# A mixture-of-experts kernel: TensorE in two short loops over fixed buffers, and results behind the weights

## The chip, the cores and the metric

The kernel runs on one core of one Trainium2 chip. The metric is the device time of one execution in microseconds (us); a profile adds the span of one execution, from its first to its last instruction, and shows what each engine did in it. In the profile PE is the matrix engine (TensorE), PEld its weight loads, DVE the vector engine, ACT the scalar engine, POOL the GpSimd engine and SP the sync engine. DMA transfers are issued by SP or by POOL and carried out by 16 DMA engines that the core has. Transfers that change the number type (float32 in memory, bfloat16 on the core) are issued by POOL here; they stand one behind another in POOL's ring. SP's transfers have a queue of their own.

## The reference

There are 8 experts. Each has 256 rows of x with 512 elements, a first weight of 512 x 2048 and a second of 2048 x 512, all float32:

```python
h = np.matmul(x, w1)      # (8, 256, 512) x (8, 512, 2048)
h = np.maximum(h, 0)
return np.matmul(h, w2)   # (8, 256, 2048) x (8, 2048, 512)
```

Each weight of an expert has 4.19 MB in memory. The 16 weights and x are 71.30 MB to read, the results 4.19 MB to write.

## The kernel before, in words

All matmuls are in bfloat16 and sum in float32. The weights are converted by the DMA that loads them. x must stand with its 512 elements on the partitions, so TensorE transposes it (line 88), and DVE and ACT copy the transposed blocks out of PSUM (lines 99 and 101).

*x.* `GROUPS` (line 35) divides the experts into four groups of 1, 1, 2 and 4. Experts 0 and 1 are loaded as float32 on SP (line 146, tile `x_f`) and cast by ACT (lines 156 and 157); groups 2 and 3 are loaded with a cast on the POOL ring (line 66, tile `x_b`). The transposes of a group stand shortly ahead of its first use; those of the last group stand between the quarters of expert 2's first layer (line 172).

*An expert.* `first_layer` (lines 103 to 123) makes the hidden layer in four quarters of 16 matmuls (line 111). Each quarter fills a PSUM tile `pt_h`, and ACT or DVE, in turn, evicts it with the relu into `ht_sb` (lines 121 and 119). `second_layer` (lines 125 to 139) has 32 matmuls of 512 columns (line 131) into two PSUM tiles `pt_o`; DVE evicts one and ACT the other into `out_sb` (lines 138 and 139), which holds the results of all experts.

*Weights.* `load_w1` (line 70) and `load_w2` (line 76) put one transfer of 4.19 MB each on the POOL ring, into pools of three buffers for w1 and three for w2 (`WB`, line 31). The second weights of experts 6 and 7 are loaded in two pieces each, so that the second layer can begin on the first piece.

*The order.* `manual_schedule` (line 49) keeps the written order on each engine; the framework sets the waits. Lines 145 to 194 are that order. Up to expert 4 the layers alternate; then the first layers of experts 5, 6 and 7 come together (lines 186 and 187), and their second layers after them (lines 192 and 193). On the ring the weights follow the same order: the last ones are w1 of experts 5, 6 and 7, then w2 of 5, 6 and 7 (lines 173 to 183).

*Results.* Result 0 is written in pieces: SP writes partitions 100 to 127 in five small transfers in mid-run (lines 169 and 170), POOL writes partitions 0 to 99 (line 191). Results 1 to 4 are one transfer on the ring (line 142, issued at line 190), so it stands behind the last weights. Results 5 to 7 are one transfer on SP at the very end (line 194), after the evictions of expert 7.

Of the kernel before, what the change touches and what calls it, by code (L numbers as in the profile page):

```python
# [7 lines left out]


@with_exitstack  # L10
def kernel(
    ctx: ExitStack,
    tc: tile.TileContext,
    x: bass.AP,
    w1: bass.AP,
    w2: bass.AP,
    out: bass.AP,
):
    nc = tc.nc
    P = 128  # L20
    bf = mybir.dt.bfloat16
    f32 = mybir.dt.float32
    relu = mybir.ActivationFunctionType.Relu

    E, C, H = x.shape
    F = w1.shape[2]
    MT = C // P
    KT1 = H // P
    KT2 = F // P
    FB = 4  # L30
    WB = 3
    CUTS = (100, 112, 116, 120, 124, 128)


    GROUPS = ((0, 1), (1, 1), (2, 2), (4, 4))


    w1_r = w1.rearrange("e (p kt) n -> e p kt n", p=P)
    w2_r = w2.rearrange("e (p kt) n -> e p kt n", p=P)
    out_r = out.rearrange("e (p mt) n -> p e mt n", p=P)  # L40

    const = ctx.enter_context(tc.tile_pool(name="const", bufs=1))
    wpool = ctx.enter_context(tc.tile_pool(name="weights", bufs=WB))
    hpool = ctx.enter_context(tc.tile_pool(name="hidden", bufs=3))
    ps_h = ctx.enter_context(tc.tile_pool(name="ps_h", bufs=2, space=bass.MemoryType.PSUM))
    ps_o = ctx.enter_context(tc.tile_pool(name="ps_o", bufs=4, space=bass.MemoryType.PSUM))


    ctx.enter_context(tc.manual_schedule())

    w1_sb, w2_sb, ht = {}, {}, {}
    group_of = {e: g for g, (e0, n) in enumerate(GROUPS) for e in range(e0, e0 + n)}
    x_f = const.tile([P, 2, MT, H], f32, name="x_f")
    x_b = [const.tile([P, n * MT, H], bf, name=f"x_b{g}") for g, (_, n) in enumerate(GROUPS)]
    xt = [const.tile([P, KT1, MT, n * P], bf, name=f"xt{g}") for g, (_, n) in enumerate(GROUPS)]
    o_sb = const.tile([P, E, MT, H], f32, name="out_sb")
    identity = const.tile([P, P], bf, name="identity")

    def x_rows(g):
        e0, n = GROUPS[g]  # L60
        return x[e0:e0 + n].rearrange("e c k -> (e c) k").rearrange(
            "(p j) k -> p j k", p=P
        )

    def load_x(g):
        nc.gpsimd.dma_start(x_b[g][:], x_rows(g))  # L66

    def load_w1(e):
        w1_sb[e] = wpool.tile([P, KT1, F], bf, tag="w1", name="w1_sb")
        nc.gpsimd.dma_start(w1_sb[e][:], w1_r[e])  # L70

    def load_w2(e):
        w2_sb[e] = wpool.tile([P, KT2, H], bf, tag="w2", name="w2_sb")
        cuts = {E - 2: (0, 8, 16), E - 1: (0, 9, 16)}.get(e, (0, KT2))
        for lo, hi in zip(cuts, cuts[1:]):
            nc.gpsimd.dma_start(w2_sb[e][:, lo:hi, :], w2_r[e, :, lo:hi, :])  # L76

    def transpose_x(g, blocks=None):


        n = GROUPS[g][1]
        J = n * MT
        KB = 8 // J
        for b in blocks if blocks is not None else range(KT1 // KB):
            pt = ps_o.tile([P, KB, J, P], bf, tag="ps_o", name="pt_tr")
            for i in range(KB):
                for j in range(J):
                    nc.tensor.transpose(  # L88
                        pt[:, i, j, :], x_b[g][:, j, b * KB + i::KT1], identity[:]
                    )  # L90
            for i in range(KB) if n > 1 else (slice(0, KB),):
                if n > 1:
                    src = pt[:, i].rearrange("p (l m) q -> p l m q", m=MT)
                    dst = xt[g][:, b * KB + i].rearrange("p m (q l) -> p l m q", l=n)
                    flip = b * KB + i
                else:
                    src, dst, flip = pt[:, i], xt[g][:], g
                if flip % 2:
                    nc.scalar.copy(dst, src)  # L99
                else:  # L100
                    nc.vector.tensor_copy(dst, src)  # L101

    def first_layer(e, between=()):
        g = group_of[e]
        i0 = (e - GROUPS[g][0]) * P
        ht[e] = hpool.tile([P, KT2, C], bf, tag="ht", name="ht_sb")
        for q in range(KT2 // FB):
            ph = ps_h.tile([P, FB, C], f32, tag="ps_h", name="pt_h")
            for i in range(FB):
                for kt in range(KT1):  # L110
                    nc.tensor.matmul(  # L111
                        ph[:, i, :],
                        w1_sb[e][:, kt, FB * q + i::KT2],
                        xt[g][:, kt, :, i0:i0 + P],
                        start=(kt == 0),
                        stop=(kt == KT1 - 1),
                    )
            if q % 2:
                nc.vector.tensor_relu(ht[e][:, FB * q:FB * (q + 1), :], ph[:])  # L119
            else:  # L120
                nc.scalar.activation(ht[e][:, FB * q:FB * (q + 1), :], ph[:], relu)  # L121
            if between:
                between.pop(0)()

    def second_layer(e):
        po = [
            ps_o.tile([P, H], f32, tag="ps_o", name=f"pt_o{mt}") for mt in range(MT)
        ]
        for kt in range(KT2):
            for mt in range(MT):  # L130
                nc.tensor.matmul(  # L131
                    po[mt][:],
                    ht[e][:, kt, mt * P:(mt + 1) * P],
                    w2_sb[e][:, kt, :],
                    start=(kt == 0),
                    stop=(kt == KT2 - 1),
                )
        nc.vector.tensor_copy(o_sb[:, e, 0, :], po[0][:])  # L138
        nc.scalar.copy(o_sb[:, e, 1, :], po[1][:])  # L139

    def store(e0, e1):
        nc.gpsimd.dma_start(out_r[:, e0:e1], o_sb[:, e0:e1])  # L142


    for e in (0, 1):
        nc.sync.dma_start(x_f[:, e], x_rows(e))
    load_w1(0)
    make_identity(nc, identity)
    load_w2(0)
    load_x(2)  # L150
    load_w1(1)
    load_w2(1)
    load_x(3)
    load_w1(2)
    load_w2(2)
    nc.scalar.copy(x_b[0][:], x_f[:, 0])  # L156
    nc.scalar.copy(x_b[1][:], x_f[:, 1])  # L157
    transpose_x(0)

    first_layer(0)  # L160
    load_w1(3)
    transpose_x(1)
    second_layer(0)
    load_w2(3)
    first_layer(1)
    load_w1(4)
    transpose_x(2)
    second_layer(1)
    for p, q in zip(CUTS, CUTS[1:]):
        nc.sync.dma_start(out_r[p:q, 0], o_sb[p:q, 0])  # L170
    load_w2(4)
    first_layer(2, [lambda kt=kt: transpose_x(3, [kt]) for kt in range(KT1)])
    load_w1(5)
    second_layer(2)
    first_layer(3)
    load_w1(6)
    second_layer(3)
    first_layer(4)
    load_w1(7)
    load_w2(5)  # L180
    load_w2(6)
    second_layer(4)
    load_w2(7)


    for e in (5, 6, 7):
        first_layer(e)


    store(1, 5)  # L190
    nc.gpsimd.dma_start(out_r[:CUTS[0], 0], o_sb[:CUTS[0], 0])  # L191
    for e in (5, 6, 7):
        second_layer(e)
    nc.sync.dma_start(out_r[:, 5:8], o_sb[:, 5:8])


# [28 lines left out]
```

## Time and profile before

| | |
|---|---|
| time, median of 3 runs | 181.9 us |
| the three runs | 181.53, 181.9, 455.66 us |
| span of the profiled execution | 180.4 us (the page gives no other time for it) |
| TensorE busy | 126.6 us, 832 matmuls |
| DVE, ACT, POOL busy | 31.8, 31.6, 12.8 us |
| read and written | 71.30 MB and 4.19 MB, 418 GB/s over the span |
| granted TensorE clock, mean | 0.930 |

How to read it: the page cuts the span into 40 equal slices and gives each engine's busy share of a slice in tenths, and the mean busy share of the 16 DMA engines; GB/s counts the bytes that arrive, so a load with a cast counts half of what it reads. The chain that ended last is followed back from the last instruction: at each step to what released it. In the list in order of time, a piece has its start, its length and what it was; "another core or an unknown queue" is a piece whose releaser the profile did not find. In a list of groups each line has the line of the kernel, the engine and operation, what was written from what, the shapes and the count, then the busy time in us and the mean of one in ns, then the idle time ahead of it and what ended it. In the list of DMA issues the last number is the median time from issue to landing in us. In a table of windows each line has the window, its length, the busy time and count for PE, PEld, DVE, ACT and POOL, then the granted clock, the DMA share and GB/s.

### The profile page before, as it was taken

The page shows a single profiled execution, that of the slowest core. Times are in us where ns is not written, and L with a number is a line of the kernel's source. Part 1 is how long each engine was busy: PE and PEld are TensorE (multiplying, and loading weights), DVE is VectorE, ACT ScalarE, POOL GpSimd, SP SyncE. Part 2 cuts the span into 40 slices and gives each one's busy share as a digit, 9 for nine tenths or more (in the row PEclk, how much of TensorE's full clock was granted, in tenths as well). Part 3 has the DMA queues.
Part 4 walks back from the last instruction along what each step waited for, and adds up shares of the span by engine and source line. Part 5 has one row for each costly group of instructions (what it writes and reads, how often), then busy time and mean ns, then how long its engine had stood idle before and what let it go on. Part 6 is the DMA issues. An engine that isn't in the chain of part 4 may idle for free.

```text
span 180.4 us, 1831 instructions
## 1 busy us (share of the span) xinstructions
PE 126.6 (70%) x832; PEld 88.8 (49%) x832; DVE 31.8 (18%) x29; ACT 31.6 (18%) x32; POOL 12.8 (7%) x28
## 2 busy tenths in 40 slices
PE   0205989159992199988769594979498967997830
PEld 0104964049840089538733591449388963443300
DVE  0100220102401018610401022012203240101010
ACT  4300240102221026612200030012222220101010
POOL 7300010100101000100100004030010000000000
PEclk9999999957999669999999997899969999999995
DMA  6999999999999999999999999999999999999995
GB/s 244 213 214 200 225 227 209 211 240 202 213 232 225 193 225 225 211 207 229 225 203 211 225 222 203 222 225 207 211 229 225 196 216 207 219 214 212 343 382 230
DMA packets 4286, 40.47 MB, mean 224 GB/s; under 512 B 440, under 2 KB 440, under 8 KB 1976
## 3 DMA queue, kind: packets, MB, share of 16 engines
q0 software_dynamic: 3536, 37.64, 95.4%
q1 hardware_dynamic: 744, 2.74, 3.9%
q8 instruction: 6, 0.10, 0.2%
HBM read 71.30 MB, written 4.19 MB: 418 GB/s over the span
## 4 chain that ended last, share of the span: by engine, by line
DMA 46%; PE 38%; another core or an unknown queue 9%; POOL 2%; issue 1%; ACT 0%; POOLq 0%
DMA w_sb<-in_w_dram 46%; PE pt_o L131 18%; PE pt_h L111 18%; PE pt_tr L88 2%; POOL w_sb L76 1%; POOL w_sb L70 0%; ACT out_sb L139 0%; POOL x_b L66 0%; POOL identity masks.py:199 0%; POOL identity masks.py:197 0%; POOLq masks.py:199 0%; POOLq L209 0%
## 5 line engine op out<-in xcount | busy, mean ns | idle before, releaser
L111 PE MATMUL pt_h<-xt,w_sb 128*128 128x256 bf16 x512 | 65.0, 292 | 31.3 <-DMA w_sb<-in_w_dram 31.3
L111 PEld LDWEIGHTS <-w_sb 128*128 128x128 bf16 x512 | 59.4, 147 | 37.4 <-DMA w_sb<-in_w_dram 34.4
L131 PE MATMUL pt_o<-w_sb,ht_sb 128*128 128x512 bf16 x256 | 58.0, 386 | 9.8 <-DMA w_sb<-in_w_dram 9.8
L131 PEld LDWEIGHTS <-ht_sb 128*128 128x128 bf16 x256 | 25.3, 99 | 41.0 <-issue 11.5
L119 DVE TENSOR_SCALAR ht_sb<-pt_h 128x1024 bf16<-128x1024 f32 x16 | 19.7, 1228 | 65.9 <-PE pt_h L111 65.9
L121 ACT ACTIVATE ht_sb<-pt_h 128x1024 bf16<-128x1024 f32 x16 | 16.5, 1031 | 69.5 <-PE pt_h L111 69.5
L139 ACT COPY out_sb<-pt_o 128x512 f32<-128x512 f32 x8 | 4.7, 586 | 62.9 <-PE pt_o L131 62.9
L138 DVE COPY out_sb<-pt_o 128x512 f32<-128x512 f32 x8 | 5.5, 692 | 57.6 <-PE pt_o L131 57.6
L70 POOL DMA_DIRECT2D w_sb<-in_w_dram x8 | 4.5, 561 | 85.2 <-PE pt_h L111 84.4
L101 DVE COPY xt<-pt_tr 128x1024 bf16<-128x1024 bf16 (+1 forms) x5 | 7.1, 1449 | 17.9 <-PE pt_tr L88 17.9
L88 PE MATMUL pt_tr<-identity,x_b 128*128 128x128 bf16 x64 | 5.3, 234 | 5.1 <-ACT x_b L156 5.1
L99 ACT COPY xt<-pt_tr 128x1024 bf16<-128x1024 bf16 (+1 forms) x5 | 7.4, 1498 | 6.5 <-PE pt_tr L88 3.9
L88 PEld LDWEIGHTS <-x_b 128*128 128x128 bf16 x64 | 4.8, 119 | 5.2 <-ACT x_b L156 5.1
L76 POOL DMA_DIRECT2D w_sb<-in_w_dram x10 | 5.4, 548 | 24.0 <-PE pt_o L131 24.0
L156 ACT ACT_TABLE_LOAD x1 | 1.3, 1283 | 0.7 <-PEq L209 0.7
L156 ACT CAST x_b<-x_f 128x1024 bf16<-128x1024 f32 x1 | 1.0, 1044 | 2.0 <-DMA x_f<-in_x_dram 2.0
L191 POOL DMA_DIRECT2D out_dram<-out_sb x1 | 0.6, 552 | 8.6 <-DMA w_sb<-in_w_dram 8.6
L66 POOL DMA_DIRECT2D x_b<-in_x_dram x2 | 1.1, 552 | 0.0
L157 ACT CAST x_b<-x_f 128x1024 bf16<-128x1024 f32 x1 | 1.0, 1047 | 0.2 <-DMA x_f<-in_x_dram 0.2
L142 POOL DMA_DIRECT2D out_dram<-out_sb x1 | 0.8, 758 | 0.3 <-issue 0.3
masks.py:199 POOL TENSOR_SCALAR_AFFINE_SELECT identity<-identity 128x128 bf16<-128x128 bf16 x1 | 0.3, 289 | 0.1
masks.py:197 POOL MEMSET identity<- 128x128 bf16 x1 | 0.2, 233 | 0.0
(4 smaller groups left out, 0.4 us busy)
## 6 DMA issues: line engine op xcount, KB each, us to landing
w_sb<-in_w_dram POOLq DMA_DIRECT2D x14, 2048.0 KB, 45.8
w_sb<-in_w_dram POOLq DMA_DIRECT2D x2, 1024.0 KB, 46.9
out_dram<-out_sb POOLq DMA_DIRECT2D x1, 2048.0 KB, 53.3
out_dram<-out_sb SPq DMA_DIRECT2D x1, 1536.0 KB, 6.1
w_sb<-in_w_dram POOLq DMA_DIRECT2D x1, 1152.0 KB, 45.0
x_f<-in_x_dram SPq DMA_DIRECT2D x2, 512.0 KB, 3.6
x_b<-in_x_dram POOLq DMA_DIRECT2D x1, 1024.0 KB, 48.4
w_sb<-in_w_dram POOLq DMA_DIRECT2D x1, 896.0 KB, 49.1
```

The source lines that it names most:

```text
L70: nc.gpsimd.dma_start(w1_sb[e][:], w1_r[e])
L76: nc.gpsimd.dma_start(w2_sb[e][:, lo:hi, :], w2_r[e, :, lo:hi, :])
L88: nc.tensor.transpose(pt[:, i, j, :], x_b[g][:, j, b * KB + i::KT1], identity[:])
L99: nc.scalar.copy(dst, src)
L101: nc.vector.tensor_copy(dst, src)
L111: nc.tensor.matmul(ph[:, i, :], w1_sb[e][:, kt, FB * q + i::KT2], xt[g][:, kt, :, i0:i0 + P], start=(kt == 0), stop=(kt == KT1 - 1),)
L119: nc.vector.tensor_relu(ht[e][:, FB * q:FB * (q + 1), :], ph[:])
L121: nc.scalar.activation(ht[e][:, FB * q:FB * (q + 1), :], ph[:], relu)
L131: nc.tensor.matmul(po[mt][:], ht[e][:, kt, mt * P:(mt + 1) * P], w2_sb[e][:, kt, :], start=(kt == 0), stop=(kt == KT2 - 1),)
L138: nc.vector.tensor_copy(o_sb[:, e, 0, :], po[0][:])
L139: nc.scalar.copy(o_sb[:, e, 1, :], po[1][:])
L156: nc.scalar.copy(x_b[0][:], x_f[:, 0])
```

## The change

The work is written again without the framework's pools and waits. What differs:

- Buffers are fixed: two for each of w1 and w2 (before: three), two for the hidden layer (three), two PSUM tiles for the first layer, two for the second, two for the transposes.
- TensorE runs two loops: one of 2 passes over 32 transposes, and one of 4 passes, each with both layers of two experts, in strict order (first layer, second layer, next expert). All addresses in a loop are the same in each pass, so x of an expert is copied by DVE to one of two fixed tiles `xe` first. Before, TensorE's stream was written out, 1666 rows of layer, transpose and weight load instructions; now it has 224 matmuls with their weight loads.
- Every wait is on a semaphore of the kernel's own. TensorE takes a counted unit from each semaphore, so that the counts are the same in each pass; SP waits for the weights in order and passes each arrival on to TensorE (`t_w`).
- x is in two halves of four experts: the first as float32 on SP (2.10 MB), cast by ACT and DVE; the second with a cast, first on the POOL ring. All transposes are done ahead of the first matmul of a layer.
- The ring's order is x, then w1 and w2 of each expert in turn. Only w2 of expert 7 has two pieces. w1(e) waits for the first layer of expert e-2, w2(e) for its second layer.
- Results 0 to 5 are one transfer on the ring behind the last weight, result 6 one more behind it, result 7 a transfer on SP. No result is written in mid-run.

The core of the new code (set-up and the eviction loops cut):

```diff
+        sp.dma_start(x_f[:], x_rows(0)).then_inc(s_x[0], 16)
+        for e in range(E):
+            sp.wait_ge(s_w1[e], 16).then_inc(t_w, 1)
+            if e < E - 1:
+                sp.wait_ge(s_w2[e], 16).then_inc(t_w, 2)
+            else:
+                sp.wait_ge(s_w2[e], 16).then_inc(t_w, 1)
+                sp.wait_ge(s_w2b, 16).then_inc(t_w, 1)
+        sp.wait_ge(s_act, E)
+        sp.wait_ge(s_dve, E)
+        sp.dma_start(out_r[:, E - 1], o_sb[:, E - 1]).then_inc(s_out[2], 16)
...
+        pool.dma_start(x_c[:], x_rows(1)).then_inc(s_x[1], 16)
+        load_w1(0)
+        load_w2(0)
...
+        load_w1(1)
+        load_w2(1)
+        for e in range(2, E):
+            pool.wait_ge(s_h, NQ * (e - 1))
+            load_w1(e)
+            pool.wait_ge(s_o, MT * (e - 1))
+            load_w2(e)
+        pool.wait_ge(s_act, E - 2)
+        pool.wait_ge(s_dve, E - 2)
+        pool.dma_start(out_r[:, :E - 2], o_sb[:, :E - 2]).then_inc(s_out[0], 16)
+        pool.wait_ge(s_act, E - 1)
+        pool.wait_ge(s_dve, E - 1)
+        pool.dma_start(out_r[:, E - 2], o_sb[:, E - 2]).then_inc(s_out[1], 16)
...
+        dve.wait_ge(s_xt, 1)
+        give_xe(0)
+        give_xe(1)
+        for e in range(E):
+            for q in range(1, NQ, 2):
+                dve.wait_ge(s_h, NQ * e + q + 1)
+                dve.tensor_relu(ht[e % 2][:, FB * q:FB * (q + 1), :], ph[1][:]).then_inc(t_hb, 1)
+            if e + 2 < E:
+                give_xe(e + 2)
+            dve.wait_ge(s_o, MT * e + 1)
+            dve.tensor_copy(o_sb[:, e, 0, :], po[0][:]).then_inc(s_dve, 1)
...
+        with pe.Fori(0, 2) as _g:
+            take(t_xb, 2)
+            for k in range(KT1):
+                take(t_pt[k % 2])
+                for j in range(J):
+                    ins = pe.transpose(pt[k % 2][:, j], x_b[:, j, k::KT1], identity[:])
+                ins.then_inc(s_tr, 1)
+
+        with pe.Fori(0, E // 2) as _i:
+            for b in range(2):
+                take(t_xe)
+                take(t_w)
+                for q in range(NQ):
+                    if q >= 2:
+                        pe.wait_ge((t_ha, t_hb)[q % 2], 1)
+                    for i in range(FB):
+                        for kt in range(KT1):
+                            ins = pe.matmul(
+                                ph[q % 2][:, i, :],
+                                w1_sb[b][:, kt, FB * q + i::KT2],
+                                xe[b][:, kt],
+                                start=(kt == 0),
+                                stop=(kt == KT1 - 1),
+                            )
+                    ins.then_inc(s_h, 1)
+                take(t_w)
+                for kt in range(KT2):
+                    if kt == 2 * FB:
+                        take(t_ha, 2)
+                    if kt == 3 * FB:
+                        take(t_hb, 2)
+                    if kt == CUT:
+                        take(t_w)
+                    for m in range(MT):
+                        ins = pe.matmul(
+                            po[m][:],
+                            ht[b][:, kt, m * P:(m + 1) * P],
+                            w2_sb[b][:, kt, :],
+                            start=(kt == 0),
+                            stop=(kt == KT2 - 1),
+                        )
+                        if kt == KT2 - 1:
+                            ins.then_inc(s_o, 1)
```

Here `s_` semaphores count up over the whole run and `t_` ones are taken down by TensorE; `s_h` counts quarters of first layers, `s_o` halves of second layers, `s_act` and `s_dve` evicted results.

More of the change, by code (lines that the diff above doesn't have):

```diff
@@ L5 @@
 from concourse import mybir
-from concourse.masks import make_identity
 from concourse._compat import with_exitstack
@@ L30 @@
     FB = 4
-    WB = 3
-    CUTS = (100, 112, 116, 120, 124, 128)
-    GROUPS = ((0, 1), (1, 1), (2, 2), (4, 4))
+    NQ = KT2 // FB
+    G = E // 2
+    J = G * MT
+    CUT = 9
     w1_r = w1.rearrange("e (p kt) n -> e p kt n", p=P)
@@ L40 @@
     out_r = out.rearrange("e (p mt) n -> p e mt n", p=P)
[L42 to L57, printed above, removed]
     def x_rows(g):
-        e0, n = GROUPS[g]
-        return x[e0:e0 + n].rearrange("e c k -> (e c) k").rearrange(
+        return x[g * G:(g + 1) * G].rearrange("e c k -> (e c) k").rearrange(
@@ L62, in x_rows @@
             "(p j) k -> p j k", p=P
         )
[L65 to L86, printed above, removed]
-                for j in range(J):
[L88 to L187, printed above, removed]
@@ L190 @@
[L190 to L194, printed above, removed]
+    x_f = nc.alloc_sbuf_tensor("x_f", [P, J, H], f32)
+    x_c = nc.alloc_sbuf_tensor("x_c", [P, J, H], bf)
+    x_b = nc.alloc_sbuf_tensor("x_b", [P, J, H], bf)
+    xt = [nc.alloc_sbuf_tensor(f"xt{g}", [P, KT1, MT, G * P], bf) for g in range(2)]
+    xe = [nc.alloc_sbuf_tensor(f"xe{b}", [P, KT1, MT, P], bf) for b in range(2)]
@@ new lines @@
+    w1_sb = [nc.alloc_sbuf_tensor(f"w1_sb{b}", [P, KT1, F], bf) for b in range(2)]
+    w2_sb = [nc.alloc_sbuf_tensor(f"w2_sb{b}", [P, KT2, H], bf) for b in range(2)]
+    ht = [nc.alloc_sbuf_tensor(f"ht_sb{b}", [P, KT2, C], bf) for b in range(2)]
+    o_sb = nc.alloc_sbuf_tensor("out_sb", [P, E, MT, H], f32)
+    identity = nc.alloc_sbuf_tensor("identity", [P, P], bf)
+    ph = [nc.alloc_psum_tensor(f"pt_h{b}", [P, FB, C], f32) for b in range(2)]
+    po = [nc.alloc_psum_tensor(f"pt_o{m}", [P, H], f32) for m in range(MT)]
```

86 lines of the change are left out of this document (added).

## The prediction

> **What bounds the kernel now.** I read the engines' shares first, then the page's strip of slices and its queues, then the chain in order of time. Everything is summed against the profiled execution, 180.4 us of span. The median of the runs is 181.9 us, so 1.5 us lie outside the span; I carry them over unchanged.
>
> ```profile
> span 180.4 us, 1831 instructions
> ...
> PE 126.6 (70%) x832; PEld 88.8 (49%) x832; DVE 31.8 (18%) x29; ACT 31.6 (18%) x32; POOL 12.8 (7%) x28
> ...
> PEclk9999999957999669999999997899969999999995
> DMA  6999999999999999999999999999999999999995
> ...
> q1 hardware_dynamic: 744, 2.74, 3.9%
> q8 instruction: 6, 0.10, 0.2%
> HBM read 71.30 MB, written 4.19 MB: 418 GB/s over the span
> ```
>
> No compute engine is above 70%, while the DMA row is full in 38 of 40 slices. The kernel must read 71.3 MB and write 4.19 MB whatever its order, and the change keeps both numbers. The chain shows the same thing as a rhythm:
>
> ```profile
> 38.11 9.30 PE pt_h L111 x64
> ...
> 82.05 7.22 PE pt_h L111 x64
> 89.27 2.42 another core or an unknown queue
> 91.73 7.07 PE pt_o L131 x32
> 98.80 2.58 another core or an unknown queue
> 101.42 7.21 PE pt_h L111 x64
> 108.63 2.45 another core or an unknown queue
> 111.12 8.57 PE pt_o L131 x32
> ...
> 120.49 49.08 DMA w_sb<-in_w_dram
> 169.62 3.20 PE pt_o L131 x14
> 172.84 0.59 ACT out_sb L139
> ```
>
> Columns are start, length, what. Each layer starts when its weight lands: 82.05, 91.73, 101.42, 111.12, so one weight per 9.69 us (4.19 MB each, 433 GB/s read). A layer takes 7.07 to 7.22 us, then TensorE sits idle for about 2.5. Even the slow ones (9.30 and 8.57 us, in slices where the PEclk strip shows 5 to 8 tenths) fit into 9.69. The last weight lands at 169.6; what follows is half a layer, an eviction and the results.
>
> ```profile
> 1.00:2.00 1.00, 0.00 (x0) 0.00 (x0) 0.00 (x0) 1.00 (x1) 0.77 (x2) 1.00 0.21 78
> 2.00:3.00 1.00, 0.00 (x0) 0.00 (x0) 0.00 (x0) 0.02 (x1) 0.93 (x3) 1.00 1.00 385
> ...
> 1.80:169.50 167.70, 123.44 (x818) 87.55 (x819) 31.15 (x28) 29.99 (x31) 12.02 (x24) 0.94 1.02 220
> 169.50:173.00 3.50, 3.18 (x14) 1.27 (x13) 0.38 (x1) 0.16 (x1) 0.00 (x0) 1.00 1.02 420
> 173.00:175.00 2.00, 0.00 (x0) 0.00 (x0) 0.31 (x1) 0.42 (x1) 0.00 (x0) 1.00 0.85 342
> 175.00:178.00 3.00, 0.00 (x0) 0.00 (x0) 0.00 (x0) 0.00 (x0) 0.00 (x0) 0.60 1.02 411
> 178.00:180.40 2.40, 0.00 (x0) 0.00 (x0) 0.00 (x0) 0.00 (x0) 0.00 (x0) 0.50 0.18 72
> ```
>
> These windows end in the granted TensorE clock, the DMA share and GB/s written (weights arrive as half as many bytes as are read, so 220 there is about the same load as 420 of results). The DMA engines run at a share of about 1 from 2 to 178 us. Only one dip lies between, 0.85 in two microseconds, before the last store comes in. So the time is fill (about 2 us), transfers, and some 2 us of completion. A change of order can win only the dip, and can lose only if it lets the rings run dry or makes the last result late.
>
> **The change, part by part.** *Loading x.* Before, SP loaded 1.05 MB as float32 and the POOL ring 3.15 MB with a cast; now 2.10 MB each. A megabyte moves from the cast path (433 GB/s read) to the float32 path (385 GB/s in the row of 2 to 3 us, about 415 for the stores): 1.05/0.385 - 1.05/0.433 = 0.30 us by the one, 0.10 by the other. I take 0.2 us, between rows that are close. It lies on the path, since DMA is the bound.
>
> *Start.* All of x for four experts now comes before the first matmul, and each cast and transpose group is bigger:
>
> ```profile
> L99 ACT COPY xt<-pt_tr 128x1024 bf16<-128x1024 bf16 x3 | 6.0, 2009 | 3.9 <-PE pt_tr L88 3.9
> L88 PE MATMUL pt_tr<-identity,x_b 128*128 128x128 bf16 x64 | 5.3, 234 | 5.1 <-ACT x_b L156 5.1
> L156 ACT CAST x_b<-x_f 128x1024 bf16<-128x1024 f32 x1 | 1.0, 1044 | 2.0 <-DMA x_f<-in_x_dram 2.0
> L119 DVE TENSOR_SCALAR ht_sb<-pt_h 128x1024 bf16<-128x1024 f32 x16 | 19.7, 1228 | 65.9 <-PE pt_h L111 65.9
> ```
>
> The 4.19 MB of x share the engines and are in by about 12 to 14 us (estimate: 1.8 + 4.19/0.4 to 0.433, and some packets of the first weight between). A cast of 2048 columns is 2 x 1.044 = 2.1 us. Four groups of eight transposes (8 x 0.234 = 1.9 us at most) alternate over two PSUM buffers with copies of 2.0 us on ACT and DVE: 6 to 7 us. Twice that, since both halves of x come before the main loop: 2 x (2.1 + 7) = 18, plus two new copies to xe (0.7 to 2.0 us each; I take 1.0). The first layer starts at 33 us, not when its weight lands (1.8 + 10 + 9.7 = 21.5). It is 11 us late, and each expert gives back 2 x 9.69 - 7.2 - 7.1 = 5.1, so the delay is gone in expert 2 or 3. The cover is those five later experts; without it 11 us would be added.
>
> *Two buffers per weight.* Weight w1(2) now waits for the first layer of expert 0, at 33 + 7.2 (or 9.3) = 40 to 42 us. The ring then still holds w1(1) and w2(1), up to 1.8 + 10 + 4 x 9.69 = 50.6. Margin: 8 to 10 us. Later, w1(e) is issued when two to three weights (20 to 29 us) are still queued, against 45.8 us from issue to landing before (rows below). Cost 0. On POOL nothing is queued behind that wait except later weights and results. If the margin were used up, every further microsecond counts in full.
>
> *Loops and relays on TensorE.* The same 768 layer matmuls with their weight loads, in four passes of one body. A relay through SP is added per weight. No row shows a branch; the nearest are the 0.01 to 0.05 us "issue" pieces of the chain and, as the far end, one transfer amid traffic, 3.6 us for a small x_f load (below). Ahead of expert 7 any such stall falls into the 2.5 us idle gap in front of each layer: a stall of 3.6 us makes a layer 1.1 us late and the next gap takes that back. Cost 0. The other sign: less code is loaded; queue 8 has 0.2% of the span, so at most 0.36 us is saved. I take 0, because a loop may load its code again.
>
> *xe copies, DVE order.* One per expert, behind the relu of expert e and ahead of its eviction, needed 10 us or more later. DVE has 2 x 1.23 + 0.69 + 2.0 at most = 5.2 us of work per 19.4. Cost 0; the last two experts have none.
>
> *Results.* Before, 112 KB of result 0 (48 + 4 x 16 KB, first rows below) went out in mid-run and 4.08 MB in the tail; now all 4.19 MB come behind the weights.
>
> ```profile
> out_dram<-out_sb SPq DMA_DIRECT2D x4, 16.0 KB
> out_dram<-out_sb SPq DMA_DIRECT2D x1, 48.0 KB
> ...
> out_dram<-out_sb SPq DMA_DIRECT2D x1, 1536.0 KB, 6.1
> x_f<-in_x_dram SPq DMA_DIRECT2D x2, 512.0 KB, 3.6
> ...
> w_sb<-in_w_dram POOLq DMA_DIRECT2D x14, 2048.0 KB, 45.8
> ```
>
> The weights end 0.115/0.42 = 0.27 us earlier and the results take 0.27 longer: 0. The dip (0.15 x 2 us = 0.30) should be filled, since 3.67 MB already stand in the ring; but the engines end unevenly and a longer tail may eat that, so it is worth 0 to -0.3; I take 0.
>
> *The last result.* In strict order, the first layer of expert 7 is no longer done ahead.
>
> ```profile
> 165.05 4.06 PE L131 MATMUL pt_o<-w_sb,ht_sb 128*128 128x512 bf16 x18 [1.22 <-DMA w_sb<-in_w_dram]
> 169.62 3.18 PE L131 MATMUL pt_o<-w_sb,ht_sb 128*128 128x512 bf16 x14 [0.50 <-DMA w_sb<-in_w_dram]
> 173.45 0.40 SPq L194 DMA_DIRECT2D out_dram<-out_sb  x1
> ```
>
> w1(7) lands at 169.6 - 9.7 = 159.9; first layer 7.2, so 167.1; 18 matmuls 4.06, 171.2; 14 matmuls 3.2, 174.4; eviction 0.6, 175.0; a store of 512 KB 3.6, so 178.6. Before, the stores landed at 173.45 + 6.1 = 179.55, and the ring's results end about there now too. So this path is hidden by 1.0 us (1.2 with the 0.2 from x). At the low clock (first layer 9.3) it would show by 0.9.
>
> Sum: 180.4 + 0.2 = 180.6 us of span, 182.1 us. Bounds of the hidden costs alone: 0.1 - 0.3 - 0.36 = -0.6 to 0.3 + 1.1 = +1.4, that is 181.3 to 183.3.
>
> **The rivals.** *TensorE late at the end (slower).* A stall inside the body of the loop, in expert 7, has no gap to fall into after w1(7) has landed. Price: 3.6 us at the far end for one fetch, and 2.1 for a first layer at the low clock; 5.7 less the hidden 1.2 is 4.5, so 186.6 us. It is slower by over 2% (3.6 us) from 4.8 us of lateness on. For it: the code must come through DMA engines that are full, and the low clock occurs (9.30). Against it: the six code transfers before cost no visible wait, and the idle gaps (2.4 to 2.6 us) at full speed left the next layer at 7.2.
>
> The Trainium skill's page "Runtime: NRT & Kernel Launch", section "Instruction fetch mechanics", speaks against loops: a taken branch to a page outside the fetched window stalls until that page has come by DMA. No trace here has such a branch. By that rule the stalls sit at the loop's end, ahead of experts 2, 4 and 6, where the 2.5 us gap and the next one take up 3.6 us, and the sum would stay at 182.1.
>
> *The ring runs dry (slower).* If the start takes over 50 us instead of 40 to 42, the third weight is issued too late. For it: the start's length is summed from rows of smaller groups. With a start 16 us longer than summed, 6 to 8 us are lost: about 189 us.
>
> *The tail shrinks (no change within 2%).* Dip filled, code traffic gone: 181.3 us. For more than 2% of gain, 3.6 us of transfers would have to vanish, while bytes and share of about 1 stay; only a higher rate of the rings could do it, 178 us, and no row shows one.
>
> **How the numbers follow.** The forecast with its small variants (181.3 to 183.3) has 0.79, TensorE late 0.15, the ring dry 0.04, a faster ring 0.02. Two per cent is about what a measurement of this kernel can tell from no change, so faster 0.02, same 0.79, slower 0.19. The range reaches from 180.8 (the low bound less the 0.4 us between the two close runs) to 186.6, the late TensorE.
>
> **What would show it.** Right: a DMA row of nines up to the last slice; layers starting 9.7 us apart from expert 3 on; the last weight landing at 169 to 170 us; the ring's results ending the chain. The start is right if the first layer begins at 30 to 36 us and w1(2) is issued by 43. Wrong: a DMA slice below 9 between 40 and 60 us (dry ring), pieces of the body in expert 7 with idle time that no weight released, or the SP store of result 7 landing more than 1 us after the ring's results.

## The result and the profile after

The changed kernel takes 184.3 us (four runs, 184.07 to 185.17), the kernel before 181.72 us (four runs; one of 455.66 us stands alone, and no later run of it comes near). The ratio is 1.0146, with a 95% interval of 1.0125 to 1.0168: slower by 2.6 us or 1.5%, inside the 2% that the prediction took as no change, clear of noise, and 2.2 us above the forecast of 182.1.

The page of the changed kernel, the lines that answer to those of before:

```profile
span 182.3 us, 1915 instructions
...
PE 127.5 (70%) x832; PEld 90.0 (49%) x832; DVE 39.4 (22%) x38; ACT 35.7 (20%) x31; POOL 11.8 (6%) x26
...
DMA  5999999999999999999999999999999999999990
...
q8 instruction: 2, 0.03, 0.1%
HBM read 71.30 MB, written 4.19 MB: 414 GB/s over the span
```

The bytes are the same and the DMA row is as full as before, with one difference: the last slice was a 5 and is now a 0. So at the end of the span there is time in which nothing is transferred. Before looking there, here is what TensorE did, in order of time (start, length, what, and in brackets the idle time ahead of it):

```profile
32.18 8.91 PE L215 MATMUL pt_h<-xe,w_sb 128*128 128x256 bf16 x64 [3.25 <-PEq L193]
40.92 7.07 PE L232 MATMUL pt_o<-w_sb,ht_sb 128*128 128x512 bf16 x32
47.83 7.15 PE L215 MATMUL pt_h<-xe,w_sb 128*128 128x256 bf16 x64
54.82 7.07 PE L232 MATMUL pt_o<-w_sb,ht_sb 128*128 128x512 bf16 x32
63.13 7.18 PE L215 MATMUL pt_h<-xe,w_sb 128*128 128x256 bf16 x64 [1.24 <-PEq L193]
72.84 8.75 PE L232 MATMUL pt_o<-w_sb,ht_sb 128*128 128x512 bf16 x32 [2.53 <-PEq L193]
82.50 7.18 PE L215 MATMUL pt_h<-xe,w_sb 128*128 128x256 bf16 x64 [0.91 <-PEq L193]
...
140.62 8.85 PE L215 MATMUL pt_h<-xe,w_sb 128*128 128x256 bf16 x64 [2.62 <-PEq L193]
150.33 7.07 PE L232 MATMUL pt_o<-w_sb,ht_sb 128*128 128x512 bf16 x32 [0.86 <-PEq L193]
```

The first layer starts at 32.18. Four layers run without a gap, then the idle gaps come back (63.13): from expert 2 on TensorE waits for weights again, and the starts lie 9.7 us apart. Slow layers (8.75, 8.85) eat part of the next gap (0.91, 0.86) and change nothing behind it. A pass of the loop begins at 63.13 and at 140.62, for two: no piece is missing there.

The stores at the end, in order of time, then in the list of DMA issues and in windows (the last two columns are DMA share and GB/s):

```profile
174.12 0.58 ACT L169 COPY out_sb<-pt_o 128x512 f32<-128x512 f32 x1 [7.63 <-PE pt_o L232]
174.73 0.35 SPq L92 DMA_DIRECT2D out_dram<-out_sb  x1
```

```profile
out_dram<-out_sb POOLq DMA_DIRECT2D x1, 512.0 KB, 19.9
out_dram<-out_sb SPq DMA_DIRECT2D x1, 512.0 KB, 4.8
```

```profile
177.00:178.00 1.00, 0.00 (x0) 0.00 (x0) 0.00 (x0) 0.00 (x0) 0.00 (x0) 1.00 0.91 373
178.00:179.00 1.00, 0.00 (x0) 0.00 (x0) 0.00 (x0) 0.00 (x0) 0.00 (x0) 1.00 0.09 37
179.00:180.00 1.00, 0.00 (x0) 0.00 (x0) 0.00 (x0) 0.00 (x0) 0.00 (x0) 0.57 0.01 4
```

The last landing is that of result 7 on SP, 174.73 + 4.8 = 179.5 us. Before, it was 173.45 + 6.1 = 179.55. By this profile the transfers end where they ended before, and the span still ends 1.9 us later. What stands behind the last landing is the end of the program, which the chain of waits does not follow. The answer for the line that the framework puts there (line 269 after, line 220 before) shows it. The columns are the engine's sequencer and operation, the count, shortest/median/longest in ns, and the first and last start in us. After:

```profile
L269 POOLq EVENT_SEMAPHORE  x4: 17/17/17, 181.7 to 182.2; - x4
L269 POOLq DRAIN  x3: 45/78/1688, 179.9 to 182.0; - x3
L269 SPq DRAIN  x3: 7/7/7, 180.2 to 181.9; - x3
```

Before:

```profile
L220 POOLq EVENT_SEMAPHORE  x4: 17/17/17, 179.7 to 180.3; - x4
L220 POOLq DRAIN  x3: 40/93/46062, 130.7 to 180.2; - x3
L220 SPq DRAIN  x3: 7/7/7, 179.6 to 179.9; - x3
```

DRAIN is an instruction of an engine's sequencer; what it does inside is not shown here, only when it begins and how long it takes. A barrier is the place where all engines wait for each other. Both kernels have the same three drains on POOL. Before, the first one began at 130.7 us, as soon as POOL had issued its last store, and took 46 us beside the transfers. So it was over at 176.8, ahead of the last landing, and the barrier was passed at 179.7, just behind SP's first drain. After, the waits are in a block of their own, and POOL has to leave that block together with all engines, when SP has seen the last store. Only then, at 179.9, does its drain begin; it takes 1.69 us with everything landed, and all engines wait for it: POOL reaches the barrier at 181.7. SP stands ready only at 180.2 (its drain), so 1.4 of the 1.69 us hold up all the others.

A second, small piece is at the start: all engines enter the block together. First issues after, then before:

```profile
0.95 0.38 SPq L82 DMA_DIRECT2D x_f<-in_x_dram  x1
1.46 0.67 POOL L106 DMA_DIRECT2D x_c<-in_x_dram  x1 [1.02 <-SPq L59]
```

```profile
0.74 0.87 SPq L146 DMA_DIRECT2D x_f<-in_x_dram  x2
1.24 0.70 POOL L70 DMA_DIRECT2D w_sb<-in_w_dram  x1 [0.79 <-POOLq L209]
```

That is 0.21 and 0.22 us.

### The profile page after: what moved, and what is told of

It reads as the page before. It is cut to its first block, busy times and chain, and to the rows that moved or that the text cites. A ratio compares the mean times of both kernels' runs of the same rounds, so it can differ in the third digit from the quotient of the medians.

```text
span 182.3 us, 1915 instructions
## 1 busy us (share of the span) xinstructions
PE 127.5 (70%) x832; PEld 90.0 (49%) x832; DVE 39.4 (22%) x38; ACT 35.7 (20%) x31; POOL 11.8 (6%) x26
## 5 line engine op out<-in xcount | busy, mean ns | idle before, releaser
L215 PE MATMUL pt_h<-xe,w_sb 128*128 128x256 bf16 x512 | 62.4, 286 | 15.8 <-PEq L193 15.8
L215 PEld LDWEIGHTS pt_h<-xe,w_sb 128*128 128x128 bf16 x512 | 58.6, 146 | 21.3 <-issue 18.9
L232 PEld LDWEIGHTS pt_o<-w_sb,ht_sb 128*128 128x128 bf16 x256 | 25.2, 99 | 40.0 <-issue 12.6
L203 PE MATMUL pt_tr<-identity,x_b 128*128 128x128 bf16 x64 | 7.5, 308 | 21.4 <-PEq L193 21.4
L203 PEld LDWEIGHTS pt_tr<-identity,x_b 128*128 128x128 bf16 x64 | 6.4, 142 | 22.3 <-issue 22.1
L147 DVE COPY xt<-pt_tr 128x1024 bf16<-128x1024 bf16 x4 | 9.7, 2431 | 7.8 <-PE pt_tr L203 7.8
L145 ACT COPY xt<-pt_tr 128x1024 bf16<-128x1024 bf16 x4 | 9.7, 2434 | 6.8 <-PE pt_tr L203 6.8
L156 ACT CAST x_b<-x_f 128x2048 bf16<-128x2048 f32 x1 | 1.9, 1898 | 9.1 <-DMA x_f<-in_x_dram 9.1
L151 DVE COPY xe<-xt 128x1024 bf16<-128x1024 bf16 x8 | 3.3, 418 | 0.9 <-ACTq L163 0.9
L160 ACT COPY x_b<-x_c 128x2048 bf16<-128x2048 bf16 x1 | 2.0, 1957 | 0.0
## 6 DMA issues: line engine op xcount, KB each, us to landing
w_sb<-in_w_dram POOLq DMA_DIRECT2D x1, 896.0 KB, 30.8
out_dram<-out_sb POOLq DMA_DIRECT2D x1, 512.0 KB, 19.9
```

Of the source, the lines that this page charges most:

```text
L145: act.copy(dst, src).then_inc(t_pt[1], 1)
L147: dve.tensor_copy(dst, src).then_inc(t_pt[0], 1)
L151: dve.tensor_copy(xe[e % 2][:], xt[g][:, :, :, i0:i0 + P]).then_inc(t_xe, 1)
L203: ins = pe.transpose(pt[k % 2][:, j], x_b[:, j, k::KT1], identity[:])
L215: ins = pe.matmul(ph[q % 2][:, i, :], w1_sb[b][:, kt, FB * q + i::KT2], xe[b][:, kt], start=(kt == 0), stop=(kt == KT1 - 1),)
L232: ins = pe.matmul(po[m][:], ht[b][:, kt, m * P:(m + 1) * P], w2_sb[b][:, kt, :], start=(kt == 0), stop=(kt == KT2 - 1),)
```

## The experiments

Three theories: *drain* (POOL's drain, late and alone, is what was lost), *loops* (TensorE's loops or their code), *tail* (the last stores end later, for which the strict order or an uneven load of the DMA engines could be the reason). The runs also list the span of each execution. Without the block the time is 1.7 to 1.9 us above it in every run that lists a span, with the block 1.7 to 2.0, and 2.0 to 2.9 in five single runs. I therefore compare median spans too: before 179.9 to 180.0, the changed kernel 182.3.

**The drain early.** One line behind POOL's last issue:

```diff
         pool.dma_start(out_r[:, E - 2], o_sb[:, E - 2]).then_inc(s_out[1], 16)
+        pool.drain()
```

> One drain more on POOL, right behind its last issue, so that it runs while the stores are still under way. Theory drain: the 1.69 us that POOL spends in its drain at 179.9 us, alone on the chip, are what the change lost; with the work done early the last drain is as short as before (0.1 us), and the span falls from 182.3 to 180.6 to 181.0 us, the time from 184.3 to 182.4 to 183.0. Theory loops (TensorE's loops or their code cost the time): no change, span 182.2 to 182.6. Theory tail (the last stores end later): no change either.

Measured: 182.51 us, median span 180.6; ratio to the kernel before 1.0049 (1.0029 to 1.007). The added drain, then POOL's barrier and last three drains:

```profile
L133 POOLq DRAIN  x1: 19215/19215/19215, 159.9 to 159.9; - x1
```

```profile
L270 POOLq EVENT_SEMAPHORE  x4: 17/17/17, 180.2 to 180.7; - x4
L270 POOLq DRAIN  x3: 39/47/78, 179.8 to 180.5; - x3
```

The drain begins at 159.9 and is over at 179.1, beside the stores; the last ones take under 0.1 us, and the barrier is reached at 180.2 instead of 181.7. One instruction more makes the kernel 1.8 us faster. *Loops* and *tail* expected nothing here. Theory drain holds.

**The framework's own drain.** The flag left out:

```diff
-    with tc.tile_critical(no_gpsimd_drain=True):
+    with tc.tile_critical():
```

> The changed kernel with the flag no_gpsimd_drain left out, so that the framework puts its own drain on POOL at the end of the block. Theory drain: if that drain stands ahead of the wait for the other engines, as in the experiment with an early drain, span 180.6 to 181.0; if behind it, 182.3 as now, and where it stands can be read in the trace. Theories loops and tail: 182.2 to 182.6.

Measured: 184.11 us, median span 182.25. The first row is the drain at the end of the block, the second the three behind it:

```profile
L59 POOLq DRAIN  x1: 1688/1688/1688, 179.7 to 179.7; - x1
```

```profile
L269 POOLq DRAIN  x3: 39/40/78, 181.5 to 182.0; - x3
```

The flag only moves the work between two places that both stand behind the wait. It takes the same 1688 ns, and it is paid once.

**The loops written out.**

```diff
-        with pe.Fori(0, 2) as _g:
+        for _g in range(2):
...
-        with pe.Fori(0, E // 2) as _i:
+        for _i in range(E // 2):
```

> Both loops of TensorE written out, same instructions in the same order, all else the same. Theory drain: the loops are not the cause, span 182.0 to 182.6 and time 184.0 to 184.6; the code queue moves about 0.1 MB again instead of 0.03. Theory loops: span 180.4 to 180.8, time 181.9 to 182.5.

Measured: 184.23 us, median span 182.15. The code traffic is back to 0.10 MB, and POOL's drain is as long as in the changed kernel:

```profile
q8 instruction: 6, 0.10, 0.2%
```

```profile
L269 POOLq DRAIN  x3: 45/78/1688, 179.7 to 181.8; - x3
```

So the loops neither cost nor save anything that four runs can tell; theory loops falls.

These two runs also answer a rival that the page of the changed kernel leaves open. The DMA records of its trace put one of its two code transfers (16 KB) at 180.8 us, inside POOL's drain, so the drain might have been a wait for code. The traces with the flag left out and with the loops written out have no code transfer there, and the drain has the same 1688 ns.

**The same loss in the kernel before.** Its last store issued by POOL:

```diff
-    nc.sync.dma_start(out_r[:, 5:8], o_sb[:, 5:8])
+    nc.gpsimd.dma_start(out_r[:, 5:8], o_sb[:, 5:8])
```

> The kernel before, with only its last store (results 5 to 7) issued by POOL instead of SP, so that POOL's drain can't begin 50 us ahead of the end but stands behind a store that lands last. Theory drain: POOL's drain now ends after the last landing, 0.5 to 1.7 us later than now, span 181.0 to 182.1 against 180.4. Theories loops and tail: nothing in this kernel loops and the bytes are the same, span 180.2 to 180.7.

Measured: 182.72 us, ratio 1.0053 (1.0039 to 1.0068), median span 180.95. The store in the list of issues, then the end:

```profile
out_dram<-out_sb POOLq DMA_DIRECT2D x1, 1536.0 KB, 5.7
```

```profile
L220 POOLq EVENT_SEMAPHORE  x4: 17/17/17, 180.5 to 181.1; - x4
L220 POOLq DRAIN  x3: 40/108/6727, 173.7 to 181.0; - x3
L220 SPq DRAIN  x3: 7/7/7, 180.0 to 180.7; - x3
```

The long drain now begins at 173.7, right at the last issue, and ends at 180.4, 0.9 us after that store has landed (173.8 + 5.7 = 179.5). The barrier that POOL passed at 179.7 is reached at 180.5. Nothing loops here, there is no block, and the bytes are the same. By the rows the barrier comes 0.8 us later, and the median span is 1.0 us longer. Not all of it needs the drain: SP now goes through its waits for the other semaphores, about 0.06 us each, behind the last landing, and its first drain stands at 180.0 instead of 179.6. That alone would have cost about 0.4 us; POOL's drain, which ends after it, sets the rest.

**Relieving the DMA engine that is last.** The kernel with the early drain, and the kernel before, each with result 7 written in two transfers cut between partitions. In the kernel before, results 5 and 6 then go out in a store of their own, so one store becomes three; the edit there, with the cut at 120:

```diff
-    nc.sync.dma_start(out_r[:, 5:8], o_sb[:, 5:8])
+    nc.sync.dma_start(out_r[:, 5:7], o_sb[:, 5:7])
+    for p, q in ((0, 120), (120, 128)):
+        nc.sync.dma_start(out_r[p:q, 7], o_sb[p:q, 7])
```

> The kernel with the early drain, and the store of result 7 on SP in two transfers, partitions 0 to 119 and 120 to 127. Theory uneven engines: the transfers end when the DMA engine that is last ends, about 1 us behind the mean; if the last one carries partitions 120 to 127, which now go to others, the end comes 0.5 to 1.1 us earlier, span 179.7 to 180.3, time 181.4 to 182.0. Rival (the last store ends late because TensorE and the eviction are late, or the last one is another engine): no gain, span 180.7 to 181.2.

> The kernel before, with result 7 taken out of its last store and written in two transfers, partitions 0 to 119 and 120 to 127. Theory uneven engines: if the last engine carries partitions 120 to 127, 0.3 to 0.9 us less, span 179.5 to 180.1, time 180.8 to 181.4. Rival (another engine is last, or two issues more on SP cost what is won): span 180.4 to 180.9, time 181.7 to 182.2.

> The same with the cut at partition 104, so that three engines are relieved. Theory uneven engines: a gain of 0.3 to 0.9 us if the last engine is one of those that carry partitions 104 to 127; together with the cut at 120 this tells which group it is in. Rival: span 180.4 to 181.0, time 181.7 to 182.3.

Measured: early drain with the cut at 120, 182.68 us (median span 180.9, against 180.6 without it); before with the cut at 120, 182.46 us (180.7); before with the cut at 104, 182.54 us (180.8), against 181.74 us (180.0) for the kernel before in the same runs. None gains. The loss of the first, 0.3 us, lies inside the scatter of its runs (spans of 180.2 to 181.1, against 180.2 to 181.0 for twelve runs with the early drain and one store, below). The kernel before loses 0.7 and 0.8 us. The single profiles (180.5, 180.3, 180.7) lie low among their own runs; read alone, the first would have looked like a gain.

The loss of the kernel before is not shown to come from the transfers. In its trace with the cut at 120, SP sees the last store at 179.0, no later than before (179.5), but then goes through seven more waits, and its first drain stands at 179.5; before, these waits had run at 173.9 to 176.2, ahead of the last landing. So the cuts do not pay, but whether they even out the load stays open, and which engine is last, if one is, was not measured.

**Semaphores.** I took the time outside the span for larger in the changed kernel, from one span of 180.4 and times of other runs. 64 unused semaphores were added to the kernel with the early drain:

```diff
+        spare = [sem(f"spare{i}") for i in range(64)]
```

> The kernel with the early drain and 64 semaphores more that nothing uses. It asks for the 0.4 to 0.6 us that the changed kernel's time stands further above its span than that of the kernel before. Theory semaphores: what is cleared around the kernel grows with their number, time 182.9 to 183.6 at a span of 180.8. Rival (their number costs nothing): 182.3 to 182.7 at 180.8.

Measured: 182.49 us, median span 180.6. Their number costs nothing that these runs can tell.

**The kernel before in place of a changed one.**

> The kernel before itself, unchanged, measured in the place of a changed kernel. In the last experiments kernels that differ from it by one store have its span (180.3 to 180.7) but 0.7 to 0.8 us more of time. If the place in the measurement makes that, this run shows a ratio of 1.002 to 1.004 at a span of 180.4; then so much has to be taken off all ratios here. If it shows 1.000, the extra microseconds outside the span belong to the changed kernels.

Measured: 181.75 against 181.72 us, ratio 1.000 (0.9991 to 1.0009), median span 180.0. The expectation's question was wrongly put: the profiled 180.4 of before is the upper end of its spans (179.7 to 180.4 in the first twelve). By medians most of the difference stands in the span.

**TensorE made late.** Repeated matmuls in the last quarter of the first layer of every second expert, on top of the early drain (N stands for the number, 9 or 27):

```diff
+                    if b == 1 and q == NQ - 1:
+                        for _ in range(N):
+                            pe.matmul(ph[q % 2][:, 0, :], w1_sb[b][:, 0, FB * q::KT2],
+                                      xe[b][:, 0], start=True, stop=True)
```

> The kernel with the early drain, and 9 matmuls repeated in the last quarter of the first layer of every second expert (their results are overwritten), so that TensorE ends about 1.0 us later (9 x 0.113) in expert 7; ahead of it the idle gaps take it. The prediction said that the path of the last result is hidden by 1.0 to 1.2 us: span 180.6 to 181.0 as without. Rival (the SP store of result 7 ended 1.1 us behind the ring's results, so TensorE's path already sets the end): span 181.6 to 182.0.

> The same with 27 matmuls, 3.05 us. With 1.0 to 1.2 us hidden the span rises by 1.9 to 2.1, to 182.6 to 183.0. If the path already sets the end: 183.6 to 184.0. If much more is hidden than predicted (the DMA engines are the bound up to 179.2): under 182.2.

Measured: 9 matmuls 182.5 us, median span 180.7 against 180.6, no loss. 27 matmuls 184.03 us, median span 182.25, 1.65 us lost; but its four spans are two pairs, 181.4 and 181.6, 182.9 and 183.1, so the median stands for none of them. The issue and the windows at the end of the run with 27:

```profile
177.63 0.35 SPq L92 DMA_DIRECT2D out_dram<-out_sb  x1
```

```profile
177.00:178.00 1.00, 0.00 (x0) 0.00 (x0) 0.49 (x1) 0.58 (x1) 0.00 (x0) 1.00 0.13 53
178.00:179.00 1.00, 0.00 (x0) 0.00 (x0) 0.00 (x0) 0.00 (x0) 0.00 (x0) 1.00 0.55 225
179.00:180.00 1.00, 0.00 (x0) 0.00 (x0) 0.00 (x0) 0.00 (x0) 0.00 (x0) 0.50 0.74 299
```

The store is issued at 177.63 instead of 174.73, the DMA engines run empty at 177 to 178 and take it up at 178 to 179. Of the 3.05 us, 1.65 show by the median, 0.8 to 2.5 in single runs; so about 1.4 us were hidden, somewhere between 0.6 and 2.3. No range of the expectation holds the median. By these traces the store itself hides the delay: issued later, it shares the DMA engines with less and lands sooner, after 4.8 us in the changed kernel, 3.9 with 9 matmuls and 2.7 with 27.

## Why the prediction was right in its range and short in its sum

*What bounds.* Right: both kernels move the same bytes at a full DMA row, and the last landing is at 179.5 us in both profiles. The last weight landed at 169.6 us (issue at 138.8, 30.8 to landing), as forecast.

*Start and two buffers.* Right, and close: first layer 33 us forecast, 32.2 measured; w1(2) was to be issued at 40 to 42 us, and POOL's timeline has it at 41.39 (the bracket is what it waited for, the first layer):

```profile
41.39 0.53 POOL L96 DMA_DIRECT2D w_sb<-in_w_dram  x1 [36.22 <-PE pt_h L215]
```

The DMA row stays full behind it, and the delay was gone in expert 2.

*Loops.* Right: cost 0. The Trainium skill's page "Runtime: NRT & Kernel Launch", section "Instruction fetch mechanics", says that a taken branch to a page that was not fetched ahead stalls. Two code transfers lie in the span of this trace, against six before. One is at 43.4 us, in the first pass of the layers' loop, the other at 180.8, behind both loops. So the later passes did not fetch their code anew, and the starts stay 9.7 us apart; the runs show no such stall for a body of this size.

*Results and the last result.* The order of events was wrong, the time right. Result 7 landed last, not the ring's results (158.5 + 19.9 = 178.4), because its store took 4.8 us and not 3.6. That is 1.1 us after the ring's results, which the prediction had named as a sign of being wrong, and the ring's results did not end the chain. Still the path of the last result did not cost the time: 9 matmuls more on it cost nothing. The path that the sum called hidden by 1.0 us is hidden by about 1.4, and that only roughly.

*x.* The 0.2 us were not isolated; no run tells them from the rest.

*The range.* Its low end has a slip of 0.1: 181.3 less 0.4 is 180.9, not 180.8.

*The step that failed* is in the first part: "So the time is fill (about 2 us), transfers, and some 2 us of completion." I carried the completion over unchanged and the sum had no term for what the change does to it. Two were needed. POOL's drain was free before only because it began at 130.7 us and was over at 176.8, while SP's store was still under way; the change took that cover away and 1.69 us appeared. And entering and leaving the block costs 0.2 us at the start and, from SP's last wait to POOL's drain (179.6 to 179.9), 0.3 at the end. From the median span of before, 180.0 (the profiled 180.4 was a high one, so my sum began 0.4 too high), that makes 180.0 + 0.2 for x + 1.7 + 0.5 = 182.4, against 182.3 measured. The early drain shows the first term (182.3 to 180.6). The block's two pieces are read from the rows and were not tried by themselves. With the drain early, leaving the block takes SP's way instead: 0.7 us from SP's last wait to the barrier (179.5 to 180.2), against 0.2 before (179.5 to 179.7). These 0.5 and the 0.2 at the start already make 0.7 us; the kernel with the early drain still has 0.6 over the kernel before, so little room is left for x.

The time was missed by 2.2 us, of which the span has 1.7 (182.3 against 180.6). The other 0.5 stand outside it. I carried over 1.5, the difference of a median and a profile of different runs; the medians of time and span differ by 1.8 in the kernel before and by 2.0 in the changed one. Why the kernels with the block have more there is open.

Nothing here beat the kernel before.

None of the rivals occurred: TensorE was not late, the ring was not dry, and the tail did not shrink. The measured 184.3 us lies outside the small variants (181.3 to 183.3). Only the slow case that I priced at 186.6 made the range hold it, for a reason that was not the true one: that is luck.

## What to carry to other kernels

When a kernel is bound by its transfers, read the end of the program as a stage of its own: which engine does its last duties after the last landing, and what they hid behind before. In these kernels a drain on the engine that issues transfers was free when it ran beside them and another queue's store landed last; put it right after that engine's last issue when a block or a barrier would otherwise hold it back. Beginning early is not enough: with the last store itself on POOL, the drain began at the last issue and still ended 0.9 us after the landing. Compare spans by medians over runs where differences are under 1%.

## What the runs showed of the hardware that I had not expected

- POOL's drain takes 1.69 us when it begins with everything landed (1688 ns in three kernels), and under 0.1 us when one has been done before. A drain that begins while POOL's transfers are under way ended 0.9 to 1.0 us after the last of them had landed: 176.8 against 175.8 in the kernel before, 180.4 against 179.5 with its last store on POOL, 179.1 against 178.2 with the early drain.
- Waits on SP cost about 0.06 us each, and their order matters at the end: with the cut at 120, seven of them behind the last landing took 0.4 us. Cutting the last store at partition 120 or 104 gained nothing.
- The layers' loop, two experts per pass, ran its four passes with one or two code transfers, and written out there were six in the span; neither moved the time.
